# Sixteen more chunks of gelu values computed between the second half's key projections, and rows paced by PE time

## The chip, the cores and the metric

The kernel runs on one core of a Trainium2 chip. The metric is device time of one execution in microseconds (us). The kernel before was timed in three runs: 3147.74, 3150.47 and 3153.35 us, median 3150.47. The profile is of one execution that took 3139.63 us, with a span of 3137.8 us from its first to its last instruction. Engines: PE (matrix products), DVE (vector), ACT (activations), POOL (GpSimd, which here issues gathers), SP (which here issues most of the transfers). A PE matmul here streams up to 512 columns.

## The reference, cut to what matters

One transformer layer on 1024 tokens of width 1024: adaptive norm, windowed attention and a short convolution, a merge, a second norm, and then a mixture of 16384 experts (`peer`), followed by a last norm. Everything around the change is in `peer`:

```
qh = (t @ w_q)                     # keys: 8 heads x 2 parts x 128
s  = qh . sub_keys                 # 128 scores for each head and part
s_top, i_top = top_k(s, 16)        # then the best 16 of 16 x 16 sums
g  = softmax(best); idx = 128 * i1 + i2
act = gelu(u_tab[idx] . t)         # 8 heads x 16 experts for each token
out = sum((g * act) * v_tab[idx])
```

An expert is numbered by a pair (i1, i2) of 128 x 128. A chunk is the 128 experts of one i1.

## The kernel before

**Two ways to the experts.** For the first half of the tokens (512) the kernel is dense: for each of the 128 chunks it computes gelu(u . h) for all 128 experts and all 512 tokens on PE, multiplies it with the gates (zero for experts not chosen) and adds the product with v to the output. For the second half, 384 tokens use the dense gates with v as well, but take gelu(u . h) from gathered rows: `dots(t)` gathers, for each of the 128 slots of 128 tokens, a row of u for each token (an indirect DMA, issued by POOL in `row`, L904, four row buffers) and DVE forms the dot product. The last 128 tokens of the second half gather rows of v too (`rows_out`).

**Stages.** Attention and merges come first. `stage2(1)` is the second half's merge, second norm and key projections; while it runs, `run_side` weaves in `gates(0)`, which selects experts for the first half and expands their gates to dense form in DRAM (`select`, `build_g`, `expand`; DVE makes one-hot tiles `e`, `ah`, `al`, PE multiplies them into `fbank`, ACT copies to `ge` at L994, and a 1 MB `gd<-ge` store follows for each 16 tokens). Inside `stage2(1)`, `early_u` (L780) computes the gelu values of the first three chunks (UPRE = 3) and stores them in DRAM (`ged`), before the norm's eight `modulate` steps. Then sixteen key projections follow, each 24 matmuls of 512 columns, with `scores` (small matmuls, and some twenty DVE top-k steps) one projection later, and `natural`, which turns the second half's activations for the gathers, beside the first eight. The weights of all these projections come through `weight` (L152): a float32 load into one of two `w32` buffers, split by ACT and DVE into high and low halves in one of four `whl` buffers, or, where the split was stored earlier, a load into `whl` alone. The key weights are of the second kind, the u weights of the first.

**The dense loop.** `dense` (L1170) makes 32 groups of 4 chunks for the first half, then 32 for the second. A chunk step of the first half loads u, splits it (`uh` on ACT, `ul` on DVE), runs 24 matmuls into `ups`, applies gelu on ACT, multiplies with the gates on DVE (`gel`), and splits v and the product (`vl`, `wdl` on DVE). Chunks 0 to 2 load `gel` from `ged` instead. After each chunk step come two output steps, each 12 matmuls for one of 8 output blocks of the group before (`res` stays in PSUM for five blocks, `vps` is added to `acc` by DVE for three).

**Pacing.** `run_side` (L1046) walks the dense loop's 376 steps of the first half and issues side work after each step. Rows: `due += rate`, the same for each step, rate (512 - 34) / 361 = 1.32. Gates of the second half (`gates_stream`): one step for each main step until the first `select` is done, and then 0.072 for each us of PE time by the program's own estimate (columns / 2370). What is left of the gates after the last of the 376 steps is issued at once. A second `run_side` does the second half's 384 steps with the rest of the rows, 162 / 374 = 0.433 for each step; rows left after that are issued before `last_group`. Side work is queued behind an anchor instruction of DVE, and the compile-time scheduler may move ready work forward.

The gates of the second half need the dot products of their tokens first (`ndots`). In their pool, `ge` has one buffer, so the next 16 tokens' copies wait until a `gd<-ge` store has read it; in `gates(0)` it has two.

Of the kernel before, what the change touches and what calls it, by code (L numbers as in the profile page):

```python
# [8 lines left out]
F32 = mybir.dt.float32  # L9
# [12 lines left out]
HALF = 512  # L22
# [9 lines left out]
LATE_DOTS = 34  # L32
GATES_B = 0.64
GATES_D = 0.072
# [2 lines left out]
DVE_ROWS = ((), tuple(range(8)), (), (1, 2, 3, 4, 5, 7))  # L37
W_FIRST = 6
UPRE = 3
SUB = 4  # L40
NGR = 128 // SUB
NRES = 5
# [67 lines left out]
class K:  # L110
# [75 lines left out]
    def setup(self):  # L186
        nc, a = self.nc, self.a
        self.g_pc, pc = self.pool("const", side="left")
        self.pc = pc
        self.id32 = pc.tile([128, 128], F32, name="id32")  # L190
        make_identity(nc.raw, self.id32)
        self.id16 = pc.tile([128, 128], F16, name="id16")
        nc.vector.tensor_copy(self.id16, self.id32)
        self.idb = pc.tile([128, 128], BF16, name="idb")
        nc.vector.tensor_copy(self.idb, self.id32)
        self.ones = pc.tile([128, 128], F32, name="ones")
        nc.vector.memset(self.ones, 1.0)
        self.eps = pc.tile([128, 1], F32, name="eps")
        nc.vector.memset(self.eps, EPS)
        self.vecs = pc.tile([128, 48 + 8 + 8 + 8 + 12 + 8], F32, name="vecs")  # L200
        nc.sync.dma_start(self.vecs, a["vecs"])
        self.bmod = self.vecs[:, 0:48]
        self.n1 = self.vecs[:, 48:56]
        self.n2 = self.vecs[:, 56:64]
        self.fg = self.vecs[:, 64:72]
        self.cw = self.vecs[:, 72:84].rearrange("p (j k) -> p j k", k=3)
        self.sink = pc.tile([128, 8], F32, name="sink")
        nc.vector.tensor_scalar(self.sink, self.vecs[:, 84:92], 2048.0, None, op0=ALU.mult)
        self.mask = pc.tile([128, 2, 128], BF16, name="mask")
        self.mod = pc.tile([128, 48, 2], F32, name="mod")  # L210
        self.a1 = pc.tile([128, 8, 2], F32, name="a1")
        self.b1 = pc.tile([128, 8, 2], F32, name="b1")
        self.cs = pc.tile([128, 8, 2], F32, name="cs")
        self.a2s = pc.tile([128, 8], F32, name="a2s")
        self.b2s = pc.tile([128, 8], F32, name="b2s")
        self.g1s = pc.tile([128, 8], F32, name="g1s")
        self.g2s = pc.tile([128, 8], F32, name="g2s")
        hc = pc.tile([128, 2, 8, CTX], F16, name="hc", tag="h2")
        self.hc = (hc[:, 0], hc[:, 1])
        self.h2h, self.h2l = [None, None], [None, None]  # L220
        self.sv = [None, pc.tile([128, 4, 2, 8, 16], F32, name="sv1")]
        self.si = [None, pc.tile([128, 4, 2, 8, 16], U32, name="si1")]
        self.h2d = self.tc.dram_tile([4, 128, D], F32, name="h2d")
        self.x1d = [self.tc.dram_tile([128, 8, HALF], F32, name=f"x1d{i}") for i in range(2)]
        self.ged = []
        self.anchor = None
        self.gd = [self.tc.dram_tile([n // 16, 128, 128, 16], F32, name=f"gd{n}") for n in (NDENSE, NMIX)]

# [476 lines left out]
    def stage2(self, hf):  # L705
        nc, a, p = self.nc, self.a, self.ps2
        full = slice(0, HALF)
        xv = a["xT"].rearrange("(k p) t -> p k t", p=128)
        mh = p.tile([128, 8, HALF], F16, name="mh", tag="mh")
        ml = p.tile([128, 8, HALF], F16, name="ml", tag="ml")  # L710
        for j in range(8):
            w = self.weight(("ga", j), a["w_in"][18 + j])
            pga = self.proj(w, self.hT[hf], full)
            sa = p.tile([128, 512], F32, name="sa", tag="sa", bufs=2)
            nc.scalar.activation(sa, pga, AF.Sigmoid, scale=2.0 ** -12)
            yield
            w = self.weight(("gv", j), a["w_in"][26 + j])
            pgv = self.proj(w, self.hT[hf], full)
            sv = p.tile([128, 512], F32, name="sgv", tag="sgv", bufs=2)
            nc.scalar.activation(sv, pgv, AF.Sigmoid, scale=2.0 ** -12)  # L720
            yield
            w = self.weight(("ac", j), a["w_ac"][j])
            pya = self.proj(w, self.aT[hf], full, nk=4)
            nc.vector.scalar_tensor_tensor(sa, pya, 2.0 ** -8, sa, op0=ALU.mult, op1=ALU.mult)
            pyc = self.proj(w, self.cT[hf], full, nk=4, k0=4)
            nc.vector.scalar_tensor_tensor(sv, pyc, 2.0 ** -8, sv, op0=ALU.mult, op1=ALU.mult)
            nc.gpsimd.tensor_tensor(sa, sa, sv, op=ALU.add)
            nc.scalar.activation(mh[:, j, :], sa, AF.Copy)
            nc.gpsimd.tensor_tensor(ml[:, j, :], sa, mh[:, j, :], op=ALU.subtract)
            yield  # L730
        yield "merged"
        if hf == 0:
            self.g_x1, self.px1 = self.pool("x1", side="right")
        x1 = self.px1.tile([128, 8, HALF], F32, name="x1", tag="x1")
        nc.sync.dma_start(x1, xv[:, :, hf * HALF:(hf + 1) * HALF])
        pss = self.bank()
        for j in range(8):
            w = self.weight(("mx", j), a["w_mx"][j])
            pm = self.proj(w, (mh, ml), full)
            nc.vector.scalar_tensor_tensor(x1[:, j, :], pm, self.g1s[:, j:j + 1], x1[:, j, :],  # L740
                                           op0=ALU.mult, op1=ALU.add)
            if j:
                self.square(pss, j - 1, x1[:, j - 1, :], self.px1, HALF)
            if j % 2:
                nc.sync.dma_start(self.x1d[hf][:, j - 1:j + 1, :], x1[:, j - 1:j + 1, :])
            yield
        self.square(pss, 7, x1[:, 7, :], self.px1, HALF)
        if hf:
            self.h2h[1] = p.tile([128, 8, HALF], F16, name="h2h1", tag="mh")
            self.h2l[1] = p.tile([128, 8, HALF], F16, name="h2l1", tag="ml")  # L750
        else:
            h2 = self.pc.tile([128, 2, 8, HALF], F16, name="h2", tag="h2")
            self.h2h[0], self.h2l[0] = h2[:, 0], h2[:, 1]
        r = self.rstd(pss, self.px1, HALF)
        if hf:
            self.early_u()
        yield "summed"
        for k in range(8):
            self.modulate(x1[:, k, :], r, self.a2s[:, k:k + 1], self.b2s[:, k:k + 1],
                          self.h2h[hf][:, k, :], self.h2l[hf][:, k, :])  # L760
            yield
        late = None
        for c in range(16):
            w = self.weight(("wq", c), a["w_q"][c])
            pq = self.proj(w, (self.h2h[hf], self.h2l[hf]), full)
            qh = self.px1.tile([128, 512], F16, name="qqh", tag="qqh", bufs=2)
            ql = self.px1.tile([128, 512], F16, name="qql", tag="qql", bufs=2)
            self.split(pq, 2.0 ** -8, qh, ql)
            if c % 8 == 0:
                skw = self.weight(("sk", c // 8), a["skT"][c // 8], scale=64.0)  # L770
            if late is not None:
                self.scores(hf, *late)
            late = (c, qh, ql, skw)
            if hf and c < 8:
                self.natural(c)
            yield
        self.scores(hf, *late)
        yield

    def early_u(self):  # L780

        nc = self.nc
        for i in range(UPRE):
            ps = self.proj(self.weight(None, self.a["u_t"][i]), (self.h2h[0], self.h2l[0]), slice(0, HALF))
            ge = self.px1.tile([128, HALF], F32, name="ge0", tag="sl", bufs=2)
            nc.scalar.activation(ge, ps, AF.Gelu, scale=2.0 ** -12)
            self.ged.append(self.tc.dram_tile([128, HALF], F32, name=f"ged{i}"))
            nc.sync.dma_start(self.ged[i], ge)

    def natural(self, k):  # L790

# [254 lines left out]
    def run_side(self, main, gates=None, grate=0.0, rows=None, rate=0.0, first=None):  # L1046
# [6 lines left out]
        for _ in main:  # L1053
            spent = pe.spent - last
            anchor, self.anchor = self.anchor or dve.last, None
            with self.tc.issue_after(anchor):
                due += rate
                while due >= 1.0:
                    due -= 1.0
                    if next(rows, False) is False:  # L1060
# [14 lines left out]
    def chunk(self, hf, i1, p, pv):  # L1075
# [5 lines left out]
        if self.gblock != (hf, i1 // GR):  # L1081
            self.gblock = hf, i1 // GR
            self.gts = []
            for q in range(2):
# [3 lines left out]
                    self.gd[hf][nb * q:nb * q + nb].rearrange("b p i t -> p b (i t)")  # L1088
                    [:, :, i1 // GR * GR * 16:(i1 // GR + 1) * GR * 16])
                self.gts.append(gt)  # L1090
        early = hf == 0 and i1 < UPRE
        if hf == 0 and not early:
            if i1 in self.u_first:
                uh, ul = self.u_first[i1]
# [185 lines left out]
    def experts(self, p, pv, acc0):  # L1280
# [2 lines left out]
        accs = [acc0, None]  # L1283
        main = self.dense(p, pv, accs)
        steps = 3 * 128 - 2 * SUB
        self.run_side(islice(main, steps), self.gates_stream(), GATES_D, rows, (512 - LATE_DOTS) / (steps - 15.0), (1, 0))
        accs[1] = self.pc.tile([128, 8, HALF], F32, name="acc1", tag="h2")
        self.run_side(self.ends(main, acc0, p), rows=rows, rate=(128 + LATE_DOTS) / 374.0)
        for _ in rows:
            pass  # L1290
        self.last_group(accs[1], p, pv)
# [140 lines left out]
```

## Time and profile before

| what | value |
| --- | --- |
| three runs, median | 3147.74 to 3153.35 us, 3150.47 us |
| profiled execution | 3139.63 us, span 3137.8 us |
| PE, DVE, ACT, POOL busy | 93%, 85%, 40%, 34% of the span |
| DMA bytes | 795.56 MB, mean 254 GB/s |
| key projections, 985 to 1124 us | DVE busy 134.17 of 139 us |
| first half's dense loop, 1124 to 2540 us | PE busy 1359.29, DVE 1255.28 of 1416 us |

Matmuls are pipelined: the profile gives each a duration that runs past the start of the next, so a busy PE can still be short of its rate. The distance between the starts of neighbouring matmuls is the better price. DVE instructions overlap their neighbours by some 0.06 us in the same way.

### The profile page before, as it was taken

To read this page: it belongs to the slowest core of one execution; us is meant where nothing else is said; L and a number is where in the kernel's file an instruction comes from. 1 tells how busy PE (TensorE), PEld (TensorE's weight loads), DVE (VectorE), ACT (ScalarE), POOL (GpSimd) and SP (SyncE) were. 2 spreads that over 40 slices of the span, in tenths; PEclk is the share of its full clock that TensorE was granted. 3 is DMA by queue.
4 is the path that set the end of the run, shared out by engine and by line. 5 is a ranking of instruction groups with operands and counts; after the bars stand their busy time and mean duration, and the time that the engine had idled before them with its cause. 6 is when DMAs were issued, how large, how long until landed. Compare 5 with 4: busy or idle time off the path is not lost.

```text
span 3137.8 us, 46209 instructions
## 1 busy us (share of the span) xinstructions
PE 2918.0 (93%) x17149; PEld 1485.6 (47%) x17149; DVE 2679.3 (85%) x5530; ACT 1270.2 (40%) x1878; POOL 1056.6 (34%) x812
## 2 busy tenths in 40 slices
PE   6899999988888989998999999999999989999988
PEld 2455555444444544443444444344444445655654
DVE  7788666699998998888798998889988988888888
ACT  4744566334555432232333332233433333433332
POOL 2200011201111005454444443444443443454544
PEclk9999999999999999999999999999999999999999
DMA  5233334653444728898899998899988979999996
GB/s 217 95 113 108 118 112 156 226 187 131 178 181 173 241 78 301 290 316 303 290 327 323 337 326 293 299 329 332 324 324 307 341 262 335 335 333 317 346 318 221
DMA packets 327186, 795.56 MB, mean 254 GB/s; under 512 B 22960, under 2 KB 147248, under 8 KB 319792
## 3 DMA queue, kind: packets, MB, share of 16 engines
q1 hardware_dynamic: 222992, 397.25, 37.1%
q0 software_dynamic: 103968, 395.36, 34.8%
q8 instruction: 134, 2.20, 0.3%
q14 instruction: 92, 0.75, 0.1%
HBM read 696.31 MB, written 96.21 MB: 253 GB/s over the span
## 4 chain that ended last, share of the span: by engine, by line
issue 19%; PE 13%; DVE 12%; DMA 11%; POOL 10%; ACT 1%; POOLq 0%; DVEq 0%; ACTq 0%; SPq 0%
POOL row L904 10%; PE res L67 5%; PE ups L67 5%; DMA row<-u,ci 4%; DMA v<-v 4%; PE vps L67 3%; DVE row L67 2%; DMA gt<-gd 2%; DVE racc L67 2%; DVE vl L67 2%; DVE wdl L67 1%; DVE acc L67 1%; DVE si L67 1%; DVE sv L67 1%; DVE eq L67 1%
## 5 line engine op out<-in xcount | busy, mean ns | idle before, releaser
L904 POOL DMA_INDIRECT row<-u,ci x512 | 674.3, 1317 | 932.3 <-DVE row L67 692.3
L67 DVE SCALAR_TENSOR_TENSOR row<-row,hn 128x1024 f32<-128x1024 f32 x512 | 618.8, 1222 | 79.1 <-DMA row<-u,ci 72.3
L67 PE MATMUL ups<-h,uh 128*128 128x512 f16 x1952 | 592.8, 386 | 20.8 <-DVE acc L67 10.4
L67 PEld LDWEIGHTS <-vh 128*128 128x128 f16 x4096 | 402.0, 99 | 375.2 <-issue 17.2
L67 PEld LDWEIGHTS <-whl 128*128 128x128 f16 x3288 | 314.6, 99 | 411.0 <-issue 84.3
L67 PE MATMUL res<-wdl,vh 128*128 128x512 f16 (+1 forms) x1280 | 457.8, 358 | 29.2 <-DVE wdl L67 29.1
L67 PE MATMUL res<-wdh,vh 128*128 128x512 f16 (+1 forms) x1280 | 456.6, 358 | 2.4 <-ACT wdh L1135 1.5
L67 PE MATMUL res<-wdh,vl 128*128 128x512 f16 (+1 forms) x1280 | 457.3, 357 | 0.0
L1109 ACT ACTIVATE vh<-v 128x1024 f16<-128x1024 f32 x248 | 258.6, 1052 | 488.9 <-DMA v<-v 404.5
L67 PE MATMUL ups<-h,ul 128*128 128x512 f16 x976 | 376.2, 385 | 22.4 <-DVE ul L67 22.4
L67 PE MATMUL bank<-hT,whl 128*128 128x512 f16 x1584 | 375.9, 387 | 16.2 <-ACT hT L331 5.7
L67 DVE SCALAR_TENSOR_TENSOR vl<-v,vh 128x1024 f16<-128x1024 f32 x248 | 299.1, 1217 | 32.7 <-ACT vh L1109 32.6
L67 PEld LDWEIGHTS <-uh 128*128 128x128 f16 x1952 | 193.1, 99 | 258.3 <-issue 37.7
L67 PEld LDWEIGHTS <-vl 128*128 128x128 f16 x2048 | 201.6, 98 | 222.2 <-issue 39.2
L904 POOL DMA_INDIRECT row<-v,ci x128 | 222.0, 1734 | 194.5 <-DVE racc L67 125.8
L67 PE MATMUL vps<-wdh,vh 128*128 128x512 f16 (+1 forms) x768 | 270.8, 353 | 0.3 <-ACT ge L994 0.3
L67 PE MATMUL vps<-wdl,vh 128*128 128x512 f16 (+1 forms) x768 | 270.8, 353 | 0.0
L67 PE MATMUL vps<-wdh,vl 128*128 128x512 f16 (+1 forms) x768 | 270.8, 353 | 0.0
L140 ACT ACTIVATE uh<-u 128x1024 f16<-128x1024 f32 x122 | 128.4, 1052 | 327.0 <-PE ups L67 274.5
L994 ACT ACTIVATE ge<-fbank 128x512 f32<-128x512 f32 x224 | 216.2, 1067 | 80.0 <-PE fbank L67 56.7
L1128 ACT ACTIVATE wdh<-gel 128x512 f16<-128x512 f32 x128 | 80.4, 630 | 344.3 <-DVE gel L67 325.5
L67 PE MATMUL fbank<-ah,e 128*128 128x128 f16 x896 | 130.9, 221 | 54.3 <-ACT ge L994 38.0
(231 smaller groups left out, 4193.5 us busy)
## 6 DMA issues: line engine op xcount, KB each, us to landing
v<-v SPq DMA_DIRECT2D x248, 512.0 KB, 5.7
u<-u_t SPq DMA_DIRECT2D x122, 512.0 KB, 6.4
gd<-ge POOLq DMA_DIRECT2D x32, 1024.0 KB, 4.4
gt<-gd SPq DMA_DIRECT2D x32, 1024.0 KB, 13.3
wm<-w_mod SPq DMA_DIRECT2D x48, 512.0 KB, 4.1
gd<-ge SPq DMA_DIRECT2D x24, 1024.0 KB, 8.2
gt<-gd SPq DMA_DIRECT2D x32, 768.0 KB, 10.6
w<-w_in SPq DMA_DIRECT2D x34, 512.0 KB, 4.0
```

What stands on the lines that cost most here:

```text
L67: r = f(*args, **kw)
L140: nc.scalar.activation(h, src, AF.Copy, scale=float(scale))
L904: self.nc.gpsimd.indirect_dma_start(out=r, out_offset=None, in_=tab, in_offset=bass.IndirectOffsetOnAxis(ap=ci[:, s:s + 1], axis=0))
L994: nc.scalar.activation(ge[:, :, o:o + 4].rearrange("p i t -> p t i"), ps, AF.Copy, scale=2.0 ** -12)
L1109: nc.scalar.activation(vh, v32, AF.Copy, scale=16.0)
L1128: nc.scalar.activation(wh, ge, AF.Copy, scale=256.0)
```

## The change

- `EARLY` is a list of 19 chunks: 0, 1, 2 as before, and 13, 20, 27, ... 118 (every seventh). After each of the sixteen key projections of the second half, `early_u` is called for one of the sixteen new chunks: load and split of u, 24 matmuls, gelu, store to DRAM.
- In the first half's dense loop, these 16 chunks load `gel` from DRAM (256 KB) instead of loading u (512 KB), splitting it and running 24 matmuls and gelu.
- The gelu tile has its own tag with two buffers (before it shared `sl`'s), and the store goes through POOL's queue instead of SP's.
- Rows are issued in proportion to a step's PE time: 478 / 1176.7 = 0.406 for each us in the first half, 162 / 499.0 = 0.325 for each us in the second. The gates' rate stays 0.072.

```diff
+EARLY = tuple(range(UPRE)) + tuple(range(13, 125, 7))
...
         if hf:
-            self.early_u()
+            self.early_u(EARLY[:UPRE])
...
             if hf and c < 8:
                 self.natural(c)
             yield
+            if hf:
+                self.early_u(EARLY[UPRE + c:UPRE + c + 1])
+                yield
...
-            ge = self.px1.tile([128, HALF], F32, name="ge0", tag="sl", bufs=2)
+            ge = self.px1.tile([128, HALF], F32, name="ge0", tag="ge0", bufs=2)
             nc.scalar.activation(ge, ps, AF.Gelu, scale=2.0 ** -12)
-            self.ged.append(self.tc.dram_tile([128, HALF], F32, name=f"ged{i}"))
-            nc.sync.dma_start(self.ged[i], ge)
+            self.ged[i] = self.tc.dram_tile([128, HALF], F32, name=f"ged{i}")
+            nc.gpsimd.dma_start(self.ged[i], ge)
...
-                due += rate
+                due += rate * spent
...
-        early = hf == 0 and i1 < UPRE
+        early = hf == 0 and i1 in EARLY
...
-        self.run_side(islice(main, steps), self.gates_stream(), GATES_D, rows, (512 - LATE_DOTS) / (steps - 15.0), (1, 0))
+        work = (256 - len(EARLY) - SUB - 6) * 24 * 512 / 2370.0
+        self.run_side(islice(main, steps), self.gates_stream(), GATES_D, rows, (512 - LATE_DOTS) / work, (1, 0))
...
-        self.run_side(self.ends(main, acc0, p), rows=rows, rate=(128 + LATE_DOTS) / 374.0)
+        work = (SUB * 512 + 123 * 384) * 24 / 2370.0
+        self.run_side(self.ends(main, acc0, p), rows=rows, rate=(128 + LATE_DOTS) / work)
```

## Rows read from the trace of the kernel before

**Rows 1.** The page: the span in us and its instructions.
```profile
span 3137.8 us, 46209 instructions
```
**Rows 2.** Five stretches: length, PE, PEld, DVE, ACT, POOL busy (instructions), clock, DMA share, GB/s.
```profile
700.00:985.00 285.00, 242.55 (x1613) 128.30 (x1614) 258.16 (x739) 148.92 (x174) 45.32 (x46) 0.97 0.43 162
985.00:1124.00 139.00, 118.54 (x896) 67.33 (x895) 134.17 (x562) 68.55 (x90) 4.29 (x8) 0.97 0.60 203
1124.00:2540.00 1416.00, 1359.29 (x6677) 630.23 (x6675) 1255.28 (x2335) 479.26 (x604) 625.50 (x476) 0.98 0.86 306
2540.00:2575.00 35.00, 27.30 (x174) 14.52 (x174) 24.54 (x43) 16.18 (x25) 10.26 (x9) 0.95 0.66 226
2575.00:3102.00 527.00, 498.17 (x2982) 295.00 (x2982) 453.21 (x674) 193.51 (x375) 268.58 (x163) 0.97 0.93 327
```
**Rows 3.** PE in order of time, 2535 us: start, duration, matmul of 512 or 128 columns.
```profile
2535.20 0.38 PE L67 MATMUL res<-wdl,vh 128*128 128x512 f16 x1
2535.41 0.38 PE L67 MATMUL res<-wdh,vl 128*128 128x512 f16 x1
2535.63 0.22 PE L67 MATMUL fbank<-ah,e 128*128 128x128 f16 x1
2535.68 0.22 PE L67 MATMUL fbank<-al,e 128*128 128x128 f16 x1
```
**Rows 4.** PE groups by form, 985 to 1124 us: count, busy, mean ns, idle before.
```profile
L67 PE MATMUL bank<-h2h,whl 128*128 128x512 f16 x254 | 80.1, 384 | 3.7 <-DMA whl<-ws_wq 2.5 <-ACT hn L799 0.8 <-ACT h2h L331 0.4
L67 PE MATMUL bank<-h2l,whl 128*128 128x512 f16 x127 | 48.8, 384 | 0.0
```
**Rows 5.** Groups by form over the span: what an early chunk costs DVE, before and after.
```profile
L67 DVE SCALAR_TENSOR_TENSOR ul<-u,uh 128x1024 f16<-128x1024 f32 x122 | 148.2, 1218 | 23.2 <-ACT uh L140 22.9
L67 DVE SCALAR_TENSOR_TENSOR whl<-w,whl 128x1024 f16<-128x1024 f32 x74 | 94.0, 1271 | 9.4 <-ACT whl L140 9.2
```
**Rows 6.** The gelu of early_u, its line's instructions: durations, first and last start.
```profile
L786 ACT ACTIVATE ge<-bank x3: 597/597/597, 973.8 to 984.3; 128x512 f32<-128x512 f32 x3
```
**Rows 7.** PE groups by form, 1124 to 2540 us: the gates' matmuls.
```profile
L67 PE MATMUL fbank<-ah,e 128*128 128x128 f16 x344 | 44.8, 222 | 12.0 <-DVE acc L67 9.7 <-DVE ah L67 2.3
L67 PE MATMUL fbank<-al,e 128*128 128x128 f16 x344 | 44.8, 222 | 0.3 <-DVE al L67 0.3
```
**Rows 8.** Waits, 1124 to 2540 us: who for whom, us in total, times, longest.
```profile
DVE row L67 <- DMA row<-u,ci: 67.6, 63, 7.8
PE ups L67 <- DVE ul L67: 22.4, 6, 7.4
PE ups L67 <- DVE acc L67: 10.4, 5, 5.0
```
**Rows 9.** DVE groups by form, 2540 to 2575 us: the gates' one-hot tiles.
```profile
L67 DVE TENSOR_TENSOR e<-iotas,ii 128x1024 f16<-128x1024 f16 x10 | 6.5, 680 | 1.8 <-PE fbank L67 1.8
```
**Rows 10.** The chain that ended last, about 2545 us: start, us, what.
```profile
2545.74 6.60 DMA gd<-ge
2552.42 3.67 ACT ge L994 x4
2556.11 4.58 DMA gd<-ge
2560.77 1.90 ACT ge L994 x2
```
**Rows 11.** SP in order of time, about 2564 us: the last gates' store, then their load.
```profile
2564.43 0.32 SPq L996 DMA_DIRECT2D gd<-ge  x1
2569.18 1.67 SPq L1086 DMA_DIRECT2D gt<-gd  x2
```
**Rows 12.** POOL in order of time: the last gathers of v rows.
```profile
3094.59 2.22 POOL L904 DMA_INDIRECT row<-v,ci  x1 [0.65 <-DVE racc L67]
3097.93 2.22 POOL L904 DMA_INDIRECT row<-v,ci  x1 [1.12 <-PE vps L67]
```
**Rows 13.** DVE in order of time: the last sums of v rows.
```profile
3102.23 2.60 DVE L67 SCALAR_TENSOR_TENSOR racc<-row,fig,racc 128x1024 f32<-128x1024 f32 x2
```

More of the change, by code (lines that the diff above doesn't have):

```diff
@@ L224, in setup @@
         self.x1d = [self.tc.dram_tile([128, 8, HALF], F32, name=f"x1d{i}") for i in range(2)]
-        self.ged = []
+        self.ged = {}
         self.anchor = None
@@ L776, in stage2, with early_u @@
             yield
+            if hf:
+                self.early_u(EARLY[UPRE + c:UPRE + c + 1])
+                yield
         self.scores(hf, *late)
         yield
-    def early_u(self):
+    def early_u(self, chunks):
         nc = self.nc
-        for i in range(UPRE):
+        for i in chunks:
             ps = self.proj(self.weight(None, self.a["u_t"][i]), (self.h2h[0], self.h2l[0]), slice(0, HALF))
-            ge = self.px1.tile([128, HALF], F32, name="ge0", tag="sl", bufs=2)
+            ge = self.px1.tile([128, HALF], F32, name="ge0", tag="ge0", bufs=2)
             nc.scalar.activation(ge, ps, AF.Gelu, scale=2.0 ** -12)
-            self.ged.append(self.tc.dram_tile([128, HALF], F32, name=f"ged{i}"))
-            nc.sync.dma_start(self.ged[i], ge)
+            self.ged[i] = self.tc.dram_tile([128, HALF], F32, name=f"ged{i}")
+            nc.gpsimd.dma_start(self.ged[i], ge)
     def natural(self, k):
```

## The prediction

> **What bounds the kernel now.** I read the page first for the span [rows 1], then a table by stretches [rows 2], because the share of busy time is an average over stages with different limits. The reader is to see three regimes. In the key projections (985 to 1124) DVE is busy 134.2 of 139 us. In the first half's dense loop (1124 to 2540) PE is busy 1359 of 1416, DVE 1255, and DMA 0.86. Between them and the second half lies a short stretch (2540 to 2575) where no engine is full.
>
> A busy PE is not yet PE at its rate, so I price matmuls by the distance of their starts: 0.21 to 0.22 us for 512 columns and 0.05 for 128 [rows 3], which is the program's own 2370 columns for each us, 0.216 and 0.054. By that the dense loop's 6677 matmuls [rows 2], of which 688 are the gates' [rows 7], are 5989 x 0.216 + 688 x 0.054 = 1331 us of PE work in 1416 us: 85 us, 6%, are stalls and time at the lower clock (0.98 granted over the stretch [rows 2]). In the key projections 381 matmuls have 512 columns [rows 4] and the other 515 are small [rows 2]: 82 + 28 = 110 us of PE work in 139, so 29 us are free. That is what the change can win there.
>
> **Part 1: sixteen projections into the key stage.** Each is 24 x 0.216 = 5.2 us of PE; the three gelus of today, two intervals over 10.5 us [rows 6], show the same pace. Sixteen are 83 us. DVE adds one weight split each, 1.27 us [rows 5], 20 us in all, ACT a split and a gelu of 0.60 [rows 6], both far below PE's time. DVE then needs 134 + 20 = 154 us, PE 110 + 83 = 193: the stage turns from DVE to PE. The time can't be under 193 us. I add the share of lost PE time that the dense loop shows, a PE-bound stretch of today, 6% or 12 us: 205 us, 66 more than 139. Bounds: 198 (5 us lost) and 214 (21 us lost, most of today's 29), that is +59 to +75.
>
> The moved DMAs: 16 loads of 512 KB on SP and 16 stores of 256 KB on POOL; the stage's DMA share is 0.60 [rows 2], and over its 205 us they add 12.6 MB to 28 MB. The loads wait on SP for a `w32` buffer, with key weights behind them; each weight has two projections, 10.4 us, to arrive. The key stage shows one such stall, 2.5 us [rows 4], inside the 5 to 21 us above. The stores wait on POOL for gelu; behind them stand only gates' stores, and nobody waits for those until the dense loop. I put them at nothing; without that cover a store costs what its wait does, and the upper bound holds it.
>
> **Part 2: sixteen projections out of the dense loop.** PE loses the same 83 us, DVE sixteen `ul` splits of 1.22 us [rows 5], 20 us, and SP 16 loads of 512 KB for 16 of 256 KB. The new `gel` loads wait on SP for one of two `gel` buffers, with later u and v loads behind them; their product is used only in the next group's outputs, so I put this at nothing, up to 10 us if those loads come late.
>
> Gates also fall out, because their rate stays 0.072 for each us of PE time, which is now less. In program order there are 4 x 12 + 3 x 20 = 108 steps. The first 13 go with the first 13 main steps, some 36 us of PE time. Before: 249 projection-sized pieces (125 projections, 124 chunks' outputs) are 1291 us, so (1291 - 36) x 0.072 = 90, and 5 steps are left. The trace agrees: 10 `e` tiles, two for each step, come after 2540 [rows 9]. After: 233 pieces are 1208 us, (1208 - 36) x 0.072 = 84, and 11 are left. Six steps less are 6 x 16 x 0.054 = 5 us of PE.
>
> So PE's work there is 1331 - 83 - 5 = 1243 us, and DVE's 1255 - 20 - 6 x 2.6 (four tiles of 0.68 [rows 9], overlapped) less some five rows = 1214. PE's lead over DVE shrinks from 76 to 29 us. The stalls are mostly PE waiting for `ul` and `acc` while DVE waits for rows: 67.6 us of DVE's idle time is for row transfers [rows 8], with the split PE needs queued behind. I take the stalls from 85 to 97 us: 1340, which is 76 less. Bounds: 65 us of stalls (even pacing helps) gives -108, and 120 (as DVE and DMA close up) gives -53.
>
> **Part 3: the boundary.** The 11 steps that are left are issued at once, and each two make one `ge` of 16 tokens in a single buffer: four copies on ACT, then the store, then the next. The chain shows 6.60 + 3.67 = 10.3 us for one and 4.58 + 1.90 + two more copies = 8.3 for the next [rows 10]. Six steps more are three of these, 25 to 31 us later. The second half's first `gt` load waits for the last store [rows 11], and the second half's first outputs for it. PE has 96 output matmuls of the last group to hide it, 20.7 us, and they are used up today: in 35 us PE is busy 27 by the profile [rows 2]. So +25; if the scheduler pulls steps forward, +15; all of it, +31.
>
> **Part 4: rows.** Before, 376 x 1.32 slots, less those of the first 13 steps and the 6 empty ones between tiles, put 474 rows of u in the first half; after, (1208 - 36) x 0.406 - 6 = 470. The second half then needs 42 + 2 + 128 = 172 slots and gets 503 x 0.325 = 163; before 38 + 2 + 128 = 168 against 384 x 0.433 = 166. So 9 rows instead of 2 come after the loop, at the end of the kernel. Today's last gathers are 3.3 us apart, 2.2 at the fastest (one gather's own time) [rows 12], and the last sum ends at 3104.8 [rows 13], 33 us before the end; seven more are 15 to 23 us. What follows the last sum (turn, norm, store of 128 tokens) runs beside the last group's outputs, 96 x 0.162 = 15.6 us of PE. I take 8 us of it as uncovered, 0 to 16.
>
> **The sum.** +66 - 76 + 25 + 8 = +23 us on the span of 3137.8, so 3161. The profiled execution took 3139.6 where the median was 3150.5, so the measured time should be 3150.5 + 23 = **3173**. The bounds together reach further than is likely; with the two large terms at their bounds in turn the range is some -35 to +55 around the sum.
>
> **Rivals.** *The dense loop's stalls shrink (faster).* Place: DVE's queue between two chunks' `ul`. Today the two output steps (5.2 us of PE) carry 2.65 rows ahead of the next `ul`, and the projection step, just as long, 1.32; paced by time both carry 2.1, so the split that PE waits for stands behind half a row less. If that takes 45 of the 85 us of stalls with it (the two waits of [rows 8] are 33, the lower clock after them up to 2% of 1416, 28 us), the sum is 23 - 12 - 45 = -34; half of it, with the tail hidden and the boundary at +15, gives 23 - 12 - 22 - 8 - 10 = -29: 3122. It decides from stalls of 68 us or less in the loop, 29 under the 97 taken. Against it: DVE gets less slack, not more, and the early chunks' cycles carry 2.1 rows, two splits' worth and gates in half the PE time. The Trainium skill, Perfetto Trace Analysis, section Optimization Strategy, says that where the most-contended engine changes between regimes, interleaving the regimes may help; by that rule the 29 free us of the key stage are a net gain, about 3122 too. The trace bears out that the regimes differ [rows 2], and no run here shows yet what is lost in the other. Chance 0.26.
>
> *The dense loop becomes DVE's or DMA's.* DMA there is at 0.86 and 306 GB/s [rows 2]; nearly the same bytes in 1340 us are 0.91, and the second half's 0.93 shows what that is like: PE's own work there is 2982 matmuls, nearly all of 384 columns, 0.162 us, some 480 of 527 us, 9% lost. 9% on 1243 is 1366, -50 instead of -76, and with the boundary at +31: +55, 3205. Chance 0.18.
>
> *The tail and the boundary are hidden* (steps and rows pulled forward by the scheduler): 66 - 76 + 10 + 0 = 0, 3150. Chance 0.14. That the change does not do what it says, I leave out: the program's order fixes it.
>
> **How the numbers follow.** The forecast has 0.42, the rivals 0.26, 0.18 and 0.14. About 0.2% (6 us) is what a measurement of this kernel can tell from no change. Faster is the first rival, with a little of the last: 0.27. Within 0.2%: most of the last and an edge of the forecast, 0.14. Slower: 0.59. The range runs from a somewhat stronger first rival, 3115, to a somewhat stronger second, 3212, and leaves out about 2 in 10.
>
> **What would show it.** Right: the key stage ends some 66 us later, with PE full and DVE near 0.75; the dense loop takes 1340 us by its first and last `ups`, with 80 to 110 us beyond its matmuls; 22 `e` tiles come after its last projection, and the next half's first `gt` load 55 to 65 us after it instead of 36; nine gathers follow the last dense output. Wrong: a key stage under 190 us, stalls under 68 us in the dense loop, or a boundary no longer than today's.

## The result and the profile after

The changed kernel took 3266.74 us (median of four runs, 3262.92 to 3275.14), the kernel before 3149.1 (four runs, 3135.29 to 3153.35): ratio 1.0374, 95% interval 1.0344 to 1.0405. The forecast was 3173 with a range up to 3212, so the sign was right and the size was not. The profiled execution has a span of 3267.6 us against 3137.8, 129.8 more; by the medians it is 117.6, mostly since the profiled execution of before lies 9.5 us below its median.

The table by stretches of the changed kernel, with the columns of [rows 2]: key stage, dense loop, boundary, second half, end.

```profile
985.00:1198.00 213.00, 199.98 (x1275) 106.11 (x1273) 159.03 (x602) 90.81 (x120) 12.97 (x24) 0.98 0.57 200
1198.00:2625.00 1427.00, 1292.74 (x6209) 591.51 (x6209) 1214.14 (x2265) 447.51 (x560) 606.39 (x472) 0.96 0.85 296
2625.00:2685.00 60.00, 40.09 (x271) 24.00 (x270) 43.17 (x70) 30.24 (x46) 13.49 (x10) 0.81 0.53 190
2685.00:3205.00 520.00, 489.09 (x2900) 288.37 (x2899) 429.52 (x646) 187.26 (x359) 246.73 (x153) 0.96 0.91 320
3205.00:3268.00 63.00, 33.22 (x195) 20.08 (x192) 46.14 (x69) 10.48 (x18) 23.75 (x19) 0.82 0.54 183
```

The key stage turned from DVE to PE, as intended (PE 200 of 213, DVE 159). In the dense loop PE has 468 matmuls less than in [rows 2] and 67 us less busy time, DVE 41 us less, and the stretch is no shorter.

For all comparisons below I cut at marks that every kernel has: the first and last `ups` matmul bound **the loop**, the last dense matmul ahead of the last group's bounds the second half, and what follows is the end. **PE's work** in the loop is its columns by 2370 for each us and 0.056 us for a small matmul (0.054 in the prediction); **lost** is the loop less that work.

| | before | after | difference | forecast |
| --- | --- | --- | --- | --- |
| 985 us to the first `ups` (key stage) | 138.8 | 212.9 | +74 | +66 |
| the loop | 1409.4 | 1414.6 | +5 | -76 |
| its PE work / lost | 1324.2 / 85.2 | 1235.9 / 178.8 | -88 / +94 | -88 / +12 |
| last `ups` to last dense matmul (boundary, second half) | 568.2 | 603.6 | +35 | +25 |
| the end | 36.4 | 51.5 | +15 | +8 |

The whole miss but some 26 us is one line: PE's work went from the loop, and lost time took its place. Of the 94 us, 74 are idle time of PE, from 56 to 130 us; in the other 20 its matmuls took longer, at a granted clock of 0.96 over the loop instead of 0.98 (the loop's lines of both kernels stand further down).

Where the loop lost it can be read chunk by chunk, from the end of one chunk's second output step to the next. The sixteen early chunks take 6.3 us each in the changed kernel (11.0 before) and so give back some 76 us. The other 107 that can be cut this way take 12.1 us each (11.3 before), and that uses it up.

Some of the waits in the changed loop (1198 to 2625 us), with who for whom, us in total, times, longest:

```profile
ACT uh L141 <- PE ups L68: 166.1, 37, 17.6
ACT uh L141 <- DMA u<-u_t: 139.3, 43, 7.5
DVE row L68 <- DMA row<-u,ci: 86.1, 54, 7.5
DVE wdl L68 <- ACT wdh L1132: 41.1, 18, 7.2
DVE ul L68 <- ACT uh L141: 32.1, 19, 4.4
PE ups L68 <- DVE acc L68: 30.1, 9, 11.7
PE ups L68 <- ACT ge L998: 22.6, 8, 8.6
DVE gel L68 <- DMA gt<-gd: 21.8, 9, 3.6
PE ups L68 <- DVE ul L68: 20.2, 7, 4.5
PE vps L68 <- ACT gel L1127: 19.0, 7, 6.9
```

And two of the kernel before (1124 to 2540 us):

```profile
ACT uh L140 <- PE ups L67: 274.5, 59, 8.8
ACT uh L140 <- DMA u<-u_t: 51.5, 22, 5.7
```

DVE waits for row transfers 86 us instead of 68, and PE three times as long for `acc`, a step of DVE's queue [rows 8]. Ahead of the split `uh` ACT waited mostly for PE before; now it waits nearly as long for the loads of u.

The boundary came as forecast. DVE's groups from 2612 to 2685 us, the gates' tiles after the last projection (10 in [rows 9]):

```profile
L68 DVE TENSOR_TENSOR e<-iotas,ii 128x1024 f16<-128x1024 f16 x22 | 15.5, 731 | 1.9 <-PE fbank L68 1.9
```

SP in order of time, the second half's first gates' load (62 us after the last `ups` at 2612.5; in [rows 11] 36 after 2533.2):

```profile
2674.94 1.07 SPq L1090 DMA_DIRECT2D gt<-gd  x2
```

And DVE in order of time, the last sums of v rows, which answer to [rows 13]:

```profile
3239.02 2.59 DVE L68 SCALAR_TENSOR_TENSOR racc<-row,fig,racc 128x1024 f32<-128x1024 f32 x2
```

### The profile page after: what moved, and what is told of

It is laid out like the page before. It is cut to its first block, busy times and chain, and to the rows that moved or that the text cites. A ratio compares the mean times of both kernels' runs of the same rounds, so it can differ in the third digit from the quotient of the medians.

```text
span 3267.6 us, 46290 instructions
## 1 busy us (share of the span) xinstructions
PE 2947.7 (90%) x17149; PEld 1495.2 (46%) x17149; DVE 2682.0 (82%) x5530; ACT 1273.4 (39%) x1878; POOL 1046.9 (32%) x831
## 4 chain that ended last, share of the span: by engine, by line
issue 17%; DMA 14%; PE 14%; DVE 12%; POOL 8%; ACT 2%; POOLq 0%; DVEq 0%; ACTq 0%; SPq 0%
POOL row L908 8%; PE bank L68 5%; DMA gt<-gd 4%; DMA v<-v 4%; DMA row<-u,ci 4%; PE ups L68 4%; PE res L68 3%; DVE row L68 3%; PE vps L68 2%; DVE racc L68 2%; DVE vl L68 2%; DVE wdl L68 1%; DVE acc L68 1%; DMA u<-u_t 1%; ACT ge L998 1%
## 5 line engine op out<-in xcount | busy, mean ns | idle before, releaser
L908 POOL DMA_INDIRECT row<-u,ci x512 | 657.9, 1285 | 909.0 <-DVE row L68 765.7
L68 PE MATMUL ups<-h,uh 128*128 128x512 f16 x1696 | 522.2, 390 | 55.3 <-DVE acc L68 30.1
L68 PEld LDWEIGHTS <-whl 128*128 128x128 f16 x3672 | 351.0, 99 | 448.7 <-issue 76.1
L68 PE MATMUL ups<-h,ul 128*128 128x512 f16 x848 | 330.4, 390 | 20.2 <-DVE ul L68 20.2
L68 PEld LDWEIGHTS <-uh 128*128 128x128 f16 x1696 | 169.5, 100 | 268.1 <-issue 78.4
L141 ACT ACTIVATE uh<-u 128x1024 f16<-128x1024 f32 x106 | 111.8, 1055 | 322.3 <-PE ups L68 166.1
```

Source lines behind the costliest of these rows:

```text
L68: r = f(*args, **kw)
L141: nc.scalar.activation(h, src, AF.Copy, scale=float(scale))
L908: self.nc.gpsimd.indirect_dma_start(out=r, out_offset=None, in_=tab, in_offset=bass.IndirectOffsetOnAxis(ap=ci[:, s:s + 1], axis=0))
```

## The experiments

My theory after the result: the loop's time is that of DVE's queue, its work and what it waits for in order, so PE's work was the wrong thing to take away. The rivals: the transfers hold it and DVE only waits for them; or the loss is made by the early chunks themselves (their load of `gel`, their place in the queues); or by the new pacing. The diffs below show only the lines that matter.

Whole times of single runs are good to some 10 to 20 us: 17 runs of the kernel before spread over 3137 to 3160, and single runs of it taken with e1 to e4 and with e17 and e18 were 3171.21 and 3171.91. So the verdicts go by the loop, which has one trace for each kernel: the four kernels with all of PE's work and ordinary chunks have loops of 1400 to 1409, the four with 16 early chunks and nothing else altered in their rows 1412 to 1419. Differences of less than some 10 us in the loop say little.

### The change taken apart

**e1_pace: the pacing alone.** From the changed kernel:

```diff
-EARLY = tuple(range(UPRE)) + tuple(range(13, 125, 7))
+EARLY = tuple(range(UPRE))
```

> The pacing alone: rows issued by PE time in both halves, but only the first three chunks early, as before. Theory A (the loss in the first half's dense loop belongs to the sixteen early chunks' short cycles): the loop stays within 15 us of the 1416 us of before, the boundary at 35 us (5 gate steps left), and only the end grows, by some 25 us, because 9 rows are left after the loop: about 3175 us in all. Rival B (the pacing itself puts rows in front of the splits that PE waits for): the loop is 60 us or more longer than 1416, and the whole 3230 us or more.

**e2_early: the sixteen chunks, with rows paced by steps as before** (the two rates go back as well).

```diff
-                due += rate * spent
+                due += rate
```

> The sixteen early chunks with the old pacing (1.32 rows after each step). Theory A: the dense loop is as long as in the changed kernel, 1427 us, or longer by up to 40 us since four rows now fall into the 5.2 us of an early chunk's cycle; the end is that of the kernel before (36 us); in all 3240 to 3280 us. Rival B: with the pacing undone the loop falls to about 1350 us and the whole to some 3165 us.

**e3_key: the key stage's part alone**, rows by steps as in e2; the loop computes the sixteen chunks once more.

```diff
-        early = hf == 0 and i1 in EARLY
+        early = hf == 0 and i1 < UPRE
```

> The key stage's part alone: the sixteen gelu tiles are computed and stored between the key projections, and the dense loop computes them again, with the old pacing. Both theories: the key stage is 213 us instead of 139, the dense loop within 15 us of 1416, boundary and end as before: about 3225 us. If the dense loop grows here too, the loss there comes from how the key stage ends and not from the early chunks or the pacing (rival C).

**e4_dense: the loop's part alone**, rows by time; nothing is added to the key stage, and the sixteen chunks load the values of one of the first three, so their gelu values are left out.

```diff
-                nc.sync.dma_start(ge, self.ged[i1])
+                nc.sync.dma_start(ge, self.ged[i1 % UPRE])
```

> The dense part alone, with the new pacing: nothing is computed between the key projections, and the sixteen chunks load one of the first three chunks' stored gelu tiles instead (this leaves sixteen projections out, so the output is not the reference's). Theory A and B: the key stage is 139 us as before and the dense loop as long as in the changed kernel, 1427 us within 15, the boundary 60 and the end 63 us: about 3190 us in all, although 83 us of PE work are gone. Rival C (the loss comes from how the key stage ends): the loop is about 1340 us and the whole some 3105.

Measured:

| | key stage | loop | lost | boundary and second half | end | whole, us |
| --- | --- | --- | --- | --- | --- | --- |
| e1_pace | 136.2 | 1400.2 | 76.0 | 586.7 | 48.4 | 3158.29 |
| e2_early | 212.1 | 1418.6 | 182.8 | 602.7 | 36.2 | 3256.43 |
| e3_key | 212.8 | 1405.8 | 81.6 | 572.2 | 35.7 | 3213.28 |
| e4_dense | 137.4 | 1413.5 | 177.7 | 612.3 | 52.6 | 3202.53 |

The key stage's part costs 74 us wherever it is (e2, e3) and does nothing else. The early chunks bring the loop nothing with either pacing (e2, e4). The pacing does no harm in the loop (e1), but with it the end is 12 to 16 us longer: seven to nine gathers come after the last dense matmul (e1, after), none with the old pacing (before, e2).

### Suspects in the loop

**e6_no_load: is it the load of `gel`?** The sixteen chunks fill `gel` by two ACT copies instead of the 256 KB load (so their gelu values are left out).

> The changed kernel, but the sixteen early chunks don't load their gelu tiles in the loop: two small ACT copies of gate values fill the tile instead (this leaves the sixteen chunks' gelu out of the product, so the output is not the reference's). Theory G: without the load the loop falls to about 1330 us, and the whole to some 3185. Theory D: the loop stays within 15 us of 1415.

Measured: loop 1411.6, lost 175.8, whole 3268.47. It is not the load.

**e7_rows_after and e8_rows_before: rows.** Every fourth gathered row of u and its dot product are left out, in the changed kernel and in the kernel before.

```diff
         for s in range(128):
+            if s % 4 == 3:
+                yield
+                continue
```

> The changed kernel without every fourth gather of a u row and its dot product (this leaves a quarter of the dot products out; the slots of the pacing stay). In the loop that is 117 rows, 145 us of DVE and 61 MB. Theory D: the loop falls by 60 us or more, to 1350 or less, towards its 1236 us of PE work. Theory G: it falls by less than 30 us.

> The kernel before, without every fourth gather of a u row and its dot product (a quarter of the dot products left out). Theory D: the loop of before was held by DVE's queue too, and falls from 1409 by 30 to 60 us towards its 1324 us of PE work, where it stops. If PE alone held it, as the prediction took it, it falls by less than 20 us.

The slots of `dot` that stay empty are set to zero first. Measured: loop 1270.3 (lost 34.5) and 1338.5 (lost 14.4); whole 3104.33 and 3070.18. With a quarter of the rows gone the change is worth 68 us in the loop, of the 88 of PE work that it takes out. So rows are what keeps it from its gain. A row is two things, a transfer and a piece of DVE's work, and the next six runs part them.

**e9_dve_less and e14_dve_before: the work without the transfer**, after and before.

```diff
             r = self.row(self.a["u"], ci, s)
+            if s % 4 == 3:
+                nc.vector.tensor_copy(dot[:, s:s + 1], r[:, 0:1])
+                yield
+                continue
```

> The changed kernel, but every fourth gathered row of u is only read for one column (a copy of one number) instead of its dot product: the gathers, their order and their bytes stay, DVE loses some 117 dots in the first half's dense loop, about 145 us of its busy time there. This leaves out a quarter of the dot products. Theory Q (the loop's time is that of DVE's queue, its own work plus what it waits for in order): the loop, 1414.6 us in the changed kernel by first to last ups matmul, falls to 1270 to 1310, as it did to 1270.3 when rows went together with their gathers. Theory T (the gathers' transfers set the loop, DVE only waits for them): the loop stays above 1385 and DVE's waits for rows grow from 86 us by over 100.

> The kernel before, with every fourth gathered row of u only read for one column instead of its dot product (this leaves out a quarter of the dot products): DVE loses about 125 us of work in the first half's dense loop, the gathers stay. Theory Q (DVE's queue held the loop before the change too): the loop falls from 1409.4 by about as much as the changed kernel's did (56 us), to 1340 to 1375. Rival P (PE's work and its own stalls held it, DVE's work beyond that was covered): 1395 or more.

**e10_dma_less and e15_dma_before: the transfer without the work.**

```diff
-            r = self.row(self.a["u"], ci, s)
+            if s % 4 != 3:
+                r = self.row(self.a["u"], ci, s)
```

> The changed kernel, but every fourth gather of a row of u is not issued, and the dot product is made with the row before it again: DVE's work stays, some 117 gathers and 61 MB fall away. This makes a quarter of the dot products from the wrong row. Theory Q: the loop loses only a part of DVE's waits for rows (86 us), so it stays between 1345 and 1415. Theory T: it falls to 1310 or less, like the run without these rows at all (1270.3).

> The kernel before, with every fourth gather of a row of u not issued and its dot product made with the row before it again (this makes a quarter of the dot products from the wrong row): 117 gathers and 61 MB fall away, DVE's work stays. Theory Q: the loop falls by nearly as much as the changed kernel's did (78 us), down to what PE's work allows (1338.5 without these rows at all): 1340 to 1365. Rival P: 1395 or more.

**e17_short_rows and e18_short_after: as many transfers, of three quarters of the bytes**, before and after.

```diff
-            r = self.row(self.a["u"], ci, s)
+            r = self.row(self.a["u"], ci, s, 768)
```

> The kernel before, with every gathered row of u cut to 768 of 1024 numbers, read from other places of the table (so the dot products are made from other and fewer numbers); a small DVE product behind each dot keeps DVE's time for a row within 0.15 us of what it was. The number of gathers and their order stay, a quarter of their bytes (some 61 MB in the loop) falls away. Theory R (bytes: the transfers' rate sets the pace): the loop falls from 1409.4 to between 1340 and 1375, like the 1347.8 with a quarter of the gathers left out. Rival L (the number of gathers, each waited for in order): 1395 or more.

> The changed kernel with the same cut: 768 of 1024 numbers of every gathered row of u, from other places of the table, and the small product behind each dot. Theory R: the loop falls from 1414.6 to between 1325 and 1365, like the 1336.3 with a quarter of the gathers left out. Rival L: 1400 or more.

The rows come from other places of the table, and the small product behind each dot keeps DVE's load: it is busy for 1252 us of the loop in e17 (1249 before) and for 1208 in e18 (1203 after the change).

The loop's line in the table by stretches, with the columns of [rows 2]. The kernel before, cut at its `ups`:

```profile
1124.00:2533.00 1409.00, 1352.29 (x6633) 626.70 (x6632) 1249.01 (x2325) 475.27 (x596) 622.01 (x472) 0.98 0.86 306
```

e14, before without a quarter of the dots:

```profile
1126.00:2529.00 1403.00, 1346.83 (x6636) 624.95 (x6635) 1129.28 (x2208) 471.90 (x597) 600.17 (x473) 0.98 0.87 308
```

e15, before without a quarter of the gathers:

```profile
1121.00:2469.00 1348.00, 1331.53 (x6634) 621.86 (x6634) 1245.48 (x2331) 474.92 (x597) 479.08 (x357) 1.00 0.81 275
```

The changed kernel, cut at its `ups`:

```profile
1198.00:2612.00 1414.00, 1283.60 (x6152) 586.69 (x6152) 1203.22 (x2246) 443.54 (x552) 600.73 (x467) 0.96 0.85 296
```

e9, after without a quarter of the dots:

```profile
1197.00:2555.00 1358.00, 1278.18 (x6154) 586.00 (x6152) 1085.85 (x2134) 439.79 (x552) 575.02 (x468) 0.97 0.87 309
```

e10, after without a quarter of the gathers:

```profile
1197.00:2533.00 1336.00, 1262.14 (x6152) 582.40 (x6152) 1201.03 (x2250) 442.46 (x553) 472.41 (x353) 0.98 0.78 269
```

In pairs, with what the change is worth in the loop under each condition:

| rows of u | loop before | loop after | the change |
| --- | --- | --- | --- |
| all | 1409.4 | 1414.6 | +5 |
| a quarter of the gathers left out, dots kept (e15, e10) | 1347.8 | 1336.3 | -12 |
| a quarter of the bytes left out (e17, e18) | 1381.9 | 1355.9 | -26 |
| a quarter of the dots left out, gathers kept (e14, e9) | 1403.0 | 1358.4 | -45 |
| both left out (e8, e7) | 1338.5 | 1270.3 | -68 |

The first two columns say what held each loop. **Before**, DVE's dots did not: e14 takes 120 us of DVE's busy time and 6 us of the loop, no more than such loops differ by, against the theory I had written down (1340 to 1375). The gathers did: e15 leaves DVE's work as it was, and the lost time falls from 85 to 24 us. **After**, both count, 56 us for the dots and 78 for the gathers; the expectations for e9 and e10 missed on either side, since each took one of the two for the cause. The last column says the same of the change: take away only the gathers, and the loop stays at 1336, with DVE busy for 1201; take away the dots, and 45 of the 88 us come back.

What the gathers cost is for the larger part their bytes after the change (59 of 78 us in e18), and for the smaller part before it (28 of 62 in e17, where both written ranges were missed): the rest goes with their number, or with POOL's work of issuing them, which no run here parts from it. e17 and e18 were taken where the kernel before ran 24 us longer than its median of 17 runs, so these two shares are good to some 10 us of loop time (an estimate: 24 of 3148 is 0.8%, and 0.8% of the loop is 11). DVE's wait for rows, who for whom, in e14, then in e15:

```profile
DVE row L67 <- DMA row<-u,ci: 78.1, 58, 7.4
```

```profile
DVE row L67 <- DMA row<-u,ci: 13.4, 8, 6.6
```

In e14 the copies that replace a dot wait 12.2 us more for their rows. With a quarter fewer gathers the wait is all but gone, and the loop is near PE's work.

### PE's work put back

If DVE and the transfers set the changed loop, PE's 88 us should cost nothing there. Four runs put 24 matmuls of 512 columns back into each of the sixteen early chunks, their result unused.

**e5_pe_back** had the program count them, so that more rows and gates were issued than in the changed kernel; it tells little: 501 rows of u fall into its loop instead of 467. **e11_pe_back2** hid them from the count, but read the split tiles of the chunk before, which could hold these back from ACT. **e13_pe_back3** uses the activations alone:

```diff
                 nc.sync.dma_start(ge, self.ged[i1])
+                ps = pv.tile([128, 512], F32, name="ups", tag="v", bufs=3)
+                for k in range(8):
+                    mm(ps, hh[:, k, 0:128], hh[:, k, :], start=k == 0, stop=False)
+                    mm(ps, hh[:, k, 128:256], hl[:, k, :], start=False, stop=False)
+                    mm(ps, hl[:, k, 0:128], hh[:, k, :], start=False, stop=k == 7)
```

**e16_pe_back_step** is the same with rows paced by steps.

> The changed kernel, with 24 matmuls put back into each of the sixteen early chunks (they repeat the product of the chunk before and nobody reads them; the output is unchanged). So the loop has its 83 us of PE work again, but no u load, no split, no gelu. Loop by its first and last u matmul, 1415 us in the changed kernel and 1409 before. Theory D (PE never set the loop's pace: DVE's queue with its rows, and the loads it frees buffers for, need some 11 us for each chunk whatever PE does): the loop stays at 1415 to 1430 us and its lost PE time falls from 179 to about 95 us. Theory G (each early chunk's gelu load stalls the loop by some 5.8 us through the two gel buffers and SP's queue): the stalls stay and the work comes on top, 1480 to 1500 us.

> The changed kernel with 24 matmuls of 512 columns put back into each of the 16 early chunks of the dense loop (on the tiles of the chunk before, their result unused), outside the program's own count of PE time, so that rows and gates are issued at the same steps as in the changed kernel. PE gets 88 us back (1235.9 to 1324.2 by columns). Theory Q (PE has that much room now and DVE's queue sets the loop): the loop stays within 1405 to 1435, the whole within 3258 to 3290. Rival S (the time that the loop lost is stalls which the missing matmuls do not cover, PE's work still adds up with them): loop 1480 to 1505, the whole about 3340 to 3360.

> The changed kernel with 24 matmuls of 512 columns put back into each of the 16 early chunks of the dense loop, now on the activations alone, which stay in place for the whole loop, so that no split tile is held; their result is unused, and rows and gates are issued at the same steps as in the changed kernel. PE's work by columns goes from 1235.9 to about 1320 us. Theory F (in the changed kernel PE's work has room and does not count): loop 1405 to 1430 against 1414.6, the whole 3255 to 3285. Rival H (PE's work still counts for about half of its length, as the 42.6 us of the run before would say): loop 1440 to 1465, the whole 3300 to 3320.

> The sixteen early chunks with rows paced by steps as before the change (loop 1418.6 when it ran without more), and 24 matmuls of 512 columns put back into each of the 16 chunks in the dense loop, their result unused; PE's work by columns goes from 1235.9 to about 1320 us. Theory W (PE's work is hidden where rows are spread evenly over the chunks, since transfers set the pace): loop 1400 to 1428. Rival H (PE's work counts for about half wherever it stands, as in the run with rows by time, 42.6 us): loop 1445 or more.

Measured: loops of 1480.3, 1457.2, 1457.2 and 1447.6; whole 3305.17, 3317.36, 3312.54 and 3284.31. The loop of e5 lies where theory G put it, but e6 has shown that the load is not the cause; that of e11 lies between its two written ranges. The theory that PE's work has room (F, W) fell: it costs 43 us of 83 (e13 against the changed kernel) and 29 (e16 against e2). More than that: e16 has PE's work, the pacing and DVE's load of the kernel before or less, and its loop is 38 us longer. So a part of the loss comes with the early chunks whatever PE does: from outputs to outputs its early chunks take 12.3 us (11.0 before) and the others 11.55 (11.34). The trace of e16 shows what one such place looks like, just behind the early chunk 55. SP in order of time:

```profile
1802.41 3.73 SPq L1110 DMA_DIRECT2D v<-v  x1
1806.24 0.39 SPq L1101 DMA_DIRECT2D u<-u_t  x1
```

DVE in order of time:

```profile
1801.17 2.35 DVE L68 SCALAR_TENSOR_TENSOR vl<-v,vh 128x1024 f16<-128x1024 f32 x2
...
1814.89 1.23 DVE L68 SCALAR_TENSOR_TENSOR vl<-v,vh 128x1024 f16<-128x1024 f32 x1 [9.63 <-ACT vh L1113]
```

ACT in order of time:

```profile
1813.80 1.06 ACT L1113 ACTIVATE vh<-v 128x1024 f16<-128x1024 f32 x1 [15.24 <-DMA v<-v]
```

Two `vl` run one behind the other, late; u and v loads share three buffers (`uv32`) that those splits free, so the next v load starts only as the first of the two ends, lands 11 us later, and ACT and then DVE stand still. In DVE's order of the changed kernel three `vl` stand in a row ahead of chunk 60's product; in the kernel before there are two at most from chunk 53 to 64. Behind the loop's start, three in a row stand at two places in the kernel before, at five in the changed one and at ten in e16; but e7 has five as well, and it loses only 34.5 us. That this order costs the 38 us is argued, not shown. At the place above, two gate loads of 1 MB, issued at 1795.65, may have held the v load back as well, and a kernel with a fourth such buffer was not run.

### A version to beat both

**e12_pace_end**: the pacing without the early chunks (`EARLY` as in e1), and the second half's rows 8% faster so that none are left for the end.

```diff
-        self.run_side(self.ends(main, acc0, p), rows=rows, rate=(128 + LATE_DOTS) / work)
+        self.run_side(self.ends(main, acc0, p), rows=rows, rate=(128 + LATE_DOTS) / (0.92 * work))
```

> The pacing alone (three early chunks as before), with the second half's rows issued 8% faster so that none are left for the end. Theory: pacing by PE time takes some 9 us out of the first half's dense loop (1400.2 against 1409.4 when it ran alone) and cost 12 us at the end only because nine or ten rows were left there; so loop about 1400, end after the last main matmul about 36, and a ratio to the kernel before of 0.995 to 0.999. Rival: the 9 us are chance or come back in the second half, ratio 0.999 to 1.003.

Measured: 3149.56 us (12 runs) against 3148.12 (17 runs), ratio 1.0003, interval 0.9981 to 1.0024. Loop 1402.6 and end 34.4 came as written, the ratio did not: it is the rival's, since the second half took back what the loop gave (593.8 against 568.2, in e1 586.7). So nothing here beats the kernel before.

## Why the prediction was right in sign and wrong in size

**Part 1, the key stage: right.** +74 lies at the bound of +75; DVE 159 and PE 200 busy in 213 us are the turn from DVE to PE that it described. The value taken, 66, was low in one term: 12 us of lost PE time, a share borrowed from the dense loop, where 213 - 193 = 20 were lost.

**Part 2, the dense loop: the step that failed.** "PE's lead over DVE shrinks from 76 to 29 us", and then "I take the stalls from 85 to 97 us" treats PE as what the loop is made of and the stalls as a small share that grows a little. PE's work did fall as worked out (88 us), but lost time rose by 94, not by 12. That the stalls of before come through rows was in the prediction, and e15 bears it out: some 60 of the 85 us go with a quarter of the gathers. What failed is that they would grow by only 12 us when PE's lead over DVE shrank to 29. In their place the runs showed that the change made the rows, and DVE's work on them above all, count for more: a quarter of DVE's dots was worth 6 us of the loop before and 56 after, a quarter of the gathers 62 and 78, and with both gone the change takes 68 us from the loop instead of adding 5 (e7, e8). That the loss runs through the order of DVE's queue is argued from these prices; DVE's idle time in the loop rose from 160 to 211 us, and only some 17 of the 51 are waits for rows. A part of the loss, 38 us with PE's work put back (e16), comes with the early chunks, and its cause stays open.

The second rival (DVE or DMA becomes the bound, chance 0.18) came nearest to this, and its price, -50 in the loop, was still 55 too good: it borrowed the second half's 9% of lost time, and the changed loop lost 12.6%. Why the two shares differ no run shows.

The first rival fell: the stalls did not shrink, lost time more than doubled. By the rule of the Trainium skill named there (Perfetto Trace Analysis, Optimization Strategy), interleaving two regimes may pay; these runs bear it out only with the rows relieved: moving the work changed the loop by +5 us as it is, and by -68 with a quarter of the rows gone.

**Part 3, the boundary: right.** 22 `e` tiles after the last projection, and the gates' load 62 us after it instead of 36, as written. The other 9 us between the last `ups` and the last dense matmul have no term in the sum; e2, with the old pacing, shows the same 34 in all, e1, with the new pacing alone, 18, so they don't add up, and what they are stays open.

**Part 4, rows: mechanism right, size off.** Nine gathers follow the last dense matmul, as worked out, and cost 15 us, not 8 (0 to 16 was the range). The last sum ends 25 us after that matmul instead of 3, and what follows the sum takes 26 us instead of 33: of 22 us only 7 were covered. e2, e3 and e12, with none left over, end in 34 to 36 us.

## What to carry to other kernels

Before work is taken from the busiest engine of a stage, ask what each of the others is worth there. Busy time did not tell it: DVE was idle for 160 of 1409 us before the change and for 211 of 1414 after it, and a quarter of its dots was worth 6 us before and 56 after. Which of two resources holds a stage is seen by relieving each alone, in the kernel before and after the change; only the pairs told that the change itself moved the bound. Work moved out of a tight loop can also change the order in which its other queues free their buffers, and here equal work put back did not give the old time again.

## What was not expected of the hardware

Over the whole loop the transfers moved 306 GB/s in the kernel before, and 308 and 309 in e14 and e9, where DVE had 120 us less to do, each at a share of 0.86 to 0.87. I had read 0.86 as room up to the 0.93 and 327 GB/s of the second half [rows 2]. These means are no limit of the transfers. Two stretches of the loop of before, with the columns of [rows 2]:

```profile
1900.00:2000.00 100.00, 93.36 (x421) 41.32 (x420) 87.49 (x167) 27.42 (x36) 42.14 (x33) 0.97 0.82 283
2100.00:2200.00 100.00, 100.00 (x536) 48.17 (x535) 92.02 (x146) 38.99 (x48) 47.65 (x35) 1.00 0.94 343
```

In the second PE was busy all the time, at a granted clock of 1.00; in the first for 93 of 100 us. The Trainium skill, DMA: Bandwidth & Descriptors, section Bandwidth, gives 341 GB/s for a transfer of 1 MB and 425 for one of 16 MB. The second stretch, a mix of row gathers with loads and stores of 512 KB and 1 MB, lies at the first of these as a mean, and single slices of 2.5 us in it (the DMA view of the kernel before, 2100 to 2200 us) reach 426. What keeps the mean of the loop below it no run here shows.
